# Recurrent heads with tokens on partitions: the norm's factor as a scale per partition, one transpose per block, one fused product

## Chip, core and metric

One core of a Trainium2 chip. The metric is the device time of one execution in microseconds (us); lower is better. TensorE is called PE, VectorE DVE, ScalarE ACT, GpSimd POOL and SyncE SP, as the profile does.

## What is computed

One step of a hybrid encoder layer for 1024 prompt tokens and 32 sample tokens, all in float32: a SwiGLU, a mixing block and a second SwiGLU. The mixing block projects the normalized input once and runs two groups of heads beside each other, a stick-breaking attention (8 heads of 64) and a gated linear recurrence, HGRN2 (4 heads, keys and values of 128 columns). The change lies in the end of the recurrent group:

```python
o_h, S_new = hgrn2_scan(q_h, k_in, heads(hi), log_f, S0, hg_chunk)       # o (B, T, 4, 128)
o_h = rms_norm(o_h, hg_out_gain) * jax.nn.silu(heads(hg))
mix = jnp.concatenate([sb_o, o_h.reshape(B, T, HG_VAL_WIDTH)], axis=-1)
x = x + mix @ w_out
```

`rms_norm` divides each token's 128 values of a head by the root of their mean square and multiplies by a gain per value.

## The kernel before

All 1056 tokens lie on the free axis for most of the program (a tile is 128 features x tokens). Tokens are worked in three groups of columns, 0 to 384, 384 to 768 and 768 to 1056 (`GROUPS`); the last one has 256 prompt and 32 sample tokens.

The mixing block is written as streams that a merger interleaves: the projection (`project_stream`, three products in float32r per pair of tiles, the `pp` rows), and for each of four head pairs the attention (`attend_stream`), the sample's attention (`sample_stream`) and one recurrent head (`hg_stream`). The projection's products are the filler: PE works them off in between, and `behind(g, g.filler)` ties a transpose to the place after the filler product that was written last. From this order a scheduler makes the sequence of each engine, by priorities and its own costs; within an engine everything then runs in that sequence. After the projection, `mix_stream` multiplies by `w_out` in the same way (`ps<-xs_a`), and after all streams `mix_units` adds the last two tiles of features (`ps<-xs_b`).

A recurrent head takes chunks of 128 tokens (8 for the prompt, one of 32 for the sample). For each it makes a new state `S` (a product `pu`, and DVE's update) and the output `po`: `vn` as the weights against `att`, then `S` against `q` (lines 1388 and 1390). The result has the 128 values on partitions and the chunk's tokens on the free axis, and ACT copies it into `f`, whose columns are free by then (line 1391).

The normalization follows in two steps for each group, skewed by one group (`skewed`). `factors` squares a group on ACT (1400), and `token_factors` (207 to 225) transposes the squares on PE in blocks of 128 (216, tile `pmc`), so that a token's squares lie along the free axis; DVE sums them (217), and POOL makes the mean plus epsilon (222) and the power -1/2 (223). `normed` spreads the factor again: `spread` (228) transposes the factor, broadcast over 128 columns, on PE (242, tile `pb`), and DVE multiplies the group by gain and factor (1408) and by the gate `sg` (1410). Then the group is stored in DRAM, or for the last head split into two float32r tiles (`to_xs`).

The attention's outputs `so` are normalized by the same helpers (`sb_out_norm`, 1036): there each token has two heads, and ACT first widens the factors (235, tile `wide`). `token_factors` also makes the factors of queries and keys (`fqn`, `fkn`). Transposes, products `pu` and `po` and several others share the three PSUM banks of the tag `px`.

Of the kernel before, what the change touches and what calls it, by code (L numbers as in the profile page):

```python
# [8 lines left out]
F32 = mybir.dt.float32  # L9
# [137 lines left out]
def gs(n):  # L147
    return slice(*GROUPS[n])


def gw(n):
    return GROUPS[n][1] - GROUPS[n][0]
# [51 lines left out]
EXP_LN, SIGMOID = "natural_log_exp_and_others", "sigmoid_and_others"  # L204


def token_factors(g, f, psp, sq, w, behind_, tokens=None):


    nc = g.nc  # L210
    nb, rows, nh = -(-w // P), min(w, P), f.shape[2]
    mc = psp.tile([P, 3, P], F32, name="pmc", tag="px", bufs=3)
    v = f[0:rows, 0:nb, 0:nh]
    with behind(g, behind_):
        for b in range(nb):
            nc.tensor.transpose(mc[0:rows, b, :], sq[:, b * P:b * P + rows], g.ident)
    nc.vector.tensor_reduce(out=v.rearrange("p b h -> p (b h)"),
                            in_=mc[0:rows, 0:nb, :].rearrange("p b (h d) -> p (b h) d", h=nh), axis=AX.X, op=ALU.add)
    wide = lambda t: t[:, :, None].broadcast_to([rows, nb, nh])
    if tokens is not None:  # L220
        nc.gpsimd.tensor_tensor(out=v, in0=v, in1=wide(g.r2[0:rows, tokens]), op=ALU.mult)
    nc.gpsimd.tensor_scalar(out=v, in0=v, scalar1=nh / P, scalar2=EPS, op0=ALU.mult, op1=ALU.add)
    nc.gpsimd.tensor_tensor(out=v, in0=v, in1=g.mh[0:rows, :, None].broadcast_to([rows, nb, nh]), op=ALU.pow)
    if tokens is not None:
        nc.gpsimd.tensor_tensor(out=v, in0=v, in1=wide(g.rc[0:rows, tokens]), op=ALU.mult)


def spread(g, psp, f, c, w):

    nh, nb = f.shape[2], -(-w // P)  # L230
    rows = min(w, P)
    if nh > 1:
        wide = g.wp.tile([P, TG], F32, name="wide", tag="xp", bufs=3)[0:rows, 0:nb * P]
        wide = wide.rearrange("p (b d) -> p b d", b=nb)
        g.nc.scalar.activation(wide.rearrange("p b (h d) -> p (b h) d", h=nh),
                               f[0:rows, c:c + nb].rearrange("p b h -> p (b h)")[:, :, None]
                               .broadcast_to([rows, nb * nh, P // nh]), AF.Copy)
    pb = psp.tile([P, 512], F32, name="pb", tag="px", bufs=3)
    for b in range(nb):
        rows = min(w - b * P, P)  # L240
        src = wide[0:rows, b] if nh > 1 else f[0:rows, c + b, 0:1].broadcast_to([rows, P])
        g.nc.tensor.transpose(pb[:, b * P:b * P + rows], src, g.ident[0:rows, 0:rows])
    return pb[:, 0:w]
# [1059 lines left out]
def hg_stream(g, m, pool, psp, hh, state, outs, out):  # L1303
# [12 lines left out]
    def cs(b, c):  # L1316
        b0, nch, L = blocks[b]
        return slice(b0 * P + c * L, b0 * P + (c + 1) * L)
# [53 lines left out]
    for b, c in [(0, c) for c in range(8)] + [(1, 0)]:  # L1372
        b0, nch, L = blocks[b]
        kT = kTs[c // 4] if b == 0 else kTs[2]
        vn = v[0:L, b0 + c, :]
        if b == 1:
            nc.sync.dma_start(outs["s_p"][0, 0, hh], S)
            S = S0
        pu = psp.tile([P, 512], F32, name="pu", tag="px", bufs=3)
        nc.tensor.matmul(pu[:, 0:P], kT[:, c % 4, :], vn, start=True, stop=True)  # L1380
        Sn = pool.tile([P, P], F32, name="S", tag="S", bufs=3)
        if S is None:
            nc.vector.tensor_copy(Sn, pu[:, 0:P])
        else:
            nc.vector.scalar_tensor_tensor(out=Sn, in0=S, scalar=f[:, cs(b, c).stop - 1:cs(b, c).stop],
                                           in1=pu[:, 0:P], op0=ALU.mult, op1=ALU.add)
        po = psp.tile([P, 512], F32, name="po", tag="px", bufs=3)
        nc.tensor.matmul(po[:, 0:L], vn, att[b][:, c, :], start=True, stop=(S is None))
        if S is not None:
            nc.tensor.matmul(po[:, 0:L], S, q[:, cs(b, c)], start=False, stop=True)  # L1390
        nc.scalar.activation(f[:, cs(b, c)], po[:, 0:L], AF.Copy)
        S = Sn
        yield 1.0
    nc.sync.dma_start(outs["s_s"][0, 0, hh], S)
    o, fo = f, {}

    def factors(n):
        w = gw(n)
        sq = pool.tile([P, TG], F32, name="sq", tag="sq", bufs=2)
        nc.scalar.activation(sq[:, 0:w], o[:, gs(n)], AF.Square)  # L1400
        if w < TG:
            nc.gpsimd.memset(sq[:, w:TG], 0.0)
        fo[n] = pool.tile([P, 3, 1], F32, name="fh", tag="fh", bufs=3)
        token_factors(g, fo[n], psp, sq, TG, g.filler)

    def normed(n):
        w = gw(n)
        nc.vector.scalar_tensor_tensor(out=o[:, gs(n)], in0=o[:, gs(n)], scalar=g.hgo[:, 0:1],
                                       in1=spread(g, psp, fo[n], 0, w), op0=ALU.mult, op1=ALU.mult)
        nc.vector.tensor_tensor(out=o[:, gs(n)], in0=o[:, gs(n)], in1=sg[:, gs(n)], op=ALU.mult)  # L1410
        out(*GROUPS[n], o[:, gs(n)])

    yield from skewed(factors, normed, range(NG))
# [485 lines left out]
```

## Time and profile before

| | |
|---|---|
| median of 3 runs | 2174.91 us (2167.78 to 2176.68) |
| the profiled execution | 2173.99 us |
| its span | 2172.3 us |
| PE busy | 2118.7 us, 98% of the span |
| DVE, ACT, POOL busy | 1469.8 us (68%), 933.2 us (43%), 585.6 us (27%) |
| granted clock of PE | 0.998 of 2.4 GHz |

Matmuls are pipelined, so a matmul's listed duration is longer than the time by which it moves the next one: what an instruction costs in a stream is read from the starts of its neighbours. In a timeline row the columns are start (us), duration (us), engine, line, operation, output<-input with shapes and number of instructions in a row; in brackets stands the engine's idle time just before and what ended it. A float32 product of 128 x 128 is two instructions, a transpose one. Of a group of instructions the row gives busy time and mean duration (ns) or the least, median and longest duration (ns).

### The profile page before, as it was taken

To read this page: it belongs to the slowest core of one execution; us is meant where nothing else is said; L and a number is where in the kernel's file an instruction comes from. 1 tells how busy PE (TensorE), PEld (TensorE's weight loads), DVE (VectorE), ACT (ScalarE), POOL (GpSimd) and SP (SyncE) were. 2 spreads that over 40 slices of the span, in tenths; PEclk is the share of its full clock that TensorE was granted. 3 is DMA by queue.
4 is the path that set the end of the run, shared out by engine and by line. 5 is a ranking of instruction groups with operands and counts; after the bars stand their busy time and mean duration, and the time that the engine had idled before them with its cause. 6 is when DMAs were issued, how large, how long until landed. Compare 5 with 4: busy or idle time off the path is not lost.

```text
span 2172.3 us, 41486 instructions
## 1 busy us (share of the span) xinstructions
PE 2118.7 (98%) x16331; PEld 2069.1 (95%) x16331; DVE 1469.8 (68%) x2548; ACT 933.2 (43%) x1812; POOL 585.6 (27%) x873
## 2 busy tenths in 40 slices
PE   7999999999999999999999999989999999999998
PEld 7999999999999999989899898989999999999998
DVE  5777666564678558778678688549677666645775
ACT  6433333233446555555564475236223233334443
POOL 1355544341000110311311311121555354320000
PEclk9999999999999999999999999999999999999999
DMA  7565555447535310120121213474775455466343
GB/s 236 179 212 169 153 171 158 155 143 264 202 126 173 106 53 26 44 70 21 54 59 29 66 61 95 142 221 151 234 216 178 158 159 164 162 217 237 122 147 124
DMA packets 328804, 307.28 MB, mean 141 GB/s; under 512 B 26592, under 2 KB 284896, under 8 KB 328608
## 3 DMA queue, kind: packets, MB, share of 16 engines
q1 hardware_dynamic: 259456, 264.75, 37.5%
q10 hardware_dynamic: 68672, 38.25, 6.1%
q8 instruction: 128, 2.10, 0.4%
q0 software_dynamic: 480, 1.62, 0.2%
q14 instruction: 68, 0.56, 0.1%
HBM read 208.46 MB, written 96.11 MB: 140 GB/s over the span
## 4 chain that ended last, share of the span: by engine, by line
PE 53%; DMA 5%; DVE 4%; POOL 1%; ACT 1%; issue 1%; SPq 0%; DVEq 0%; ACTq 0%; POOLq 0%
PE bk L384 16%; PE pp L835 14%; PE bk L699 10%; PE pl L1341 2%; PE ps L1448 2%; PE av L1111 1%; PE pt L1092 1%; DMA xd<-xp 1%; PE ps L1471 1%; PE z L1147 1%; PE z L1146 1%; DMA wraw<-in_ffn_w_in_dram 1%; DMA braw<-in_ffn_w_in_dram 1%; DVE t L1005 1%; DMA oraw<-in_ffn_w_out_dram 1%
## 5 line engine op out<-in xcount | busy, mean ns | idle before, releaser
L699 PE MATMUL bk<-tl,wh 128*128 128x256 f32 x1232 | 349.9, 285 | 0.8 <-DVE tl L657 0.8
L699 PE MATMUL bk<-th,wl 128*128 128x256 f32 x1232 | 349.3, 284 | 0.8 <-DVE wl L646 0.8
L699 PE MATMUL bk<-th,wh 128*128 128x256 f32 x1232 | 348.2, 284 | 0.1
L835 PE MATMUL pp<-xs_a,wh 128*128 128x384 f32 (+1 forms) x1008 | 258.2, 337 | 0.0
L699 PEld LDWEIGHTS bk<-tl,wh 128*128 128x128 f32 x1232 | 231.8, 188 | 1.3 <-DVE tl L657 1.2
L699 PEld LDWEIGHTS bk<-th,wl 128*128 128x128 f32 x1232 | 231.8, 188 | 1.2 <-DVE wl L646 1.0
L699 PEld LDWEIGHTS bk<-th,wh 128*128 128x128 f32 x1232 | 230.9, 188 | 0.8 <-ACT wh L645 0.3
L835 PEld LDWEIGHTS pp<-xs_a,wh 128*128 128x128 f32 x1008 | 168.7, 189 | 6.0 <-issue 4.1
L646 DVE SCALAR_TENSOR_TENSOR wl<-oraw,wh 128x1024 fp32r<-128x1024 f32 x84 | 95.5, 1137 | 107.7 <-ACT wh L645 107.7
L835 PE MATMUL pp<-xs_a,wl 128*128 128x384 f32 (+1 forms) x504 | 164.0, 325 | 0.0
L539 POOL TENSOR_TENSOR gt<-gt,b 128x256 f32<-128x256 f32 x88 | 75.2, 854 | 327.1 <-ACT gt L538 323.0
L645 ACT ACTIVATE wh<-oraw 128x1024 fp32r<-128x1024 f32 x84 | 83.7, 997 | 148.2 <-PE bk L699 128.6
L384 PE MATMUL bk<-ops_a,wh 128*128 128x272 f32 (+1 forms) x704 | 131.8, 287 | 1.3 <-ACT e L364 1.1
L538 ACT ACTIVATE gt<-gt 128x256 f32<-128x256 f32 x88 | 37.3, 424 | 219.7 <-DVE gt L505 219.7
L158 DVE TENSOR_TENSOR wl<-wraw,wh 128x512 fp32r<-128x512 f32 (+2 forms) x126 | 106.5, 859 | 31.6 <-ACT wh L157 31.1
L157 ACT ACTIVATE wh<-wraw 128x512 fp32r<-128x512 f32 (+2 forms) x126 | 89.5, 731 | 88.0 <-PE bk L384 27.8
L384 PEld LDWEIGHTS bk<-ops_a,wh 128*128 128x128 f32 x704 | 110.0, 190 | 2.2 <-ACT e L364 2.2
L543 POOL TENSOR_TENSOR gt<-gt,b 128x256 f32<-128x256 f32 x88 | 88.6, 1007 | 79.7 <-DVE b L505 68.5
L384 PE MATMUL bk<-ops_a,wl 128*128 128x272 f32 (+1 forms) x352 | 100.5, 286 | 0.1
L505 DVE TENSOR_TENSOR gt<-bk,p 128x256 f32<-128x256 f32 (+1 forms) x60 | 25.9, 432 | 110.0 <-PE bk L384 107.7
L835 PEld LDWEIGHTS pp<-xs_a,wl 128*128 128x128 f32 x504 | 94.7, 188 | 0.1
L1003 ACT ACTIVATE t<-z,minus 128x128 f32<-128x128 f32 (+2 forms) x96 | 55.4, 577 | 67.8 <-PE z L1149 48.8
(469 smaller groups left out, 6848.3 us busy)
## 6 DMA issues: line engine op xcount, KB each, us to landing
wraw<-in_ffn_w_in_dram SPq DMA_DIRECT2D x58, 512.0 KB, 4.5
oraw<-in_ffn_w_out_dram SPq DMA_DIRECT2D x94, 256.0 KB, 4.4
sd<-osum SPq DMA_DIRECT2D x44, 512.0 KB, 3.1
gd<-gt SPq DMA_DIRECT2D x42, 528.0 KB, 4.9
braw<-in_ffn_w_in_dram ACTq DMA_DIRECT2D x42, 512.0 KB, 4.3
oraw<-sd SPq DMA_DIRECT2D x40, 512.0 KB, 3.6
oraw<-in_ffn_w_out_dram SPq DMA_DIRECT2D x30, 512.0 KB, 3.3
wraw<-in_w_in_dram SPq DMA_DIRECT2D x28, 512.0 KB, 3.7
```

The lines of the kernel that those rows point to most:

```text
L157: nc.scalar.activation(hi, src, AF.Copy)
L158: return nc.vector.tensor_tensor(out=lo, in0=src, in1=hi, op=ALU.subtract)
L384: mm = g.nc.tensor.matmul(ps, wt[x][:, kk, :], xt[y][:, kk, :], start=(first and kk == 0 and n == 0), stop=(kk == HK - 1 and n == len(PASS ...
L539: nc.gpsimd.tensor_tensor(out=gt[:, 1, cc], in0=gt[:, 1, cc], in1=s["b2"], op=ALU.mult)
L543: last = nc.gpsimd.tensor_tensor(out=gt[:, 0, cc], in0=gt[:, 0, cc], in1=s["b1"], op=ALU.mult)
L645: nc.scalar.activation(h, r, AF.Copy, scale=0.5)
L646: nc.vector.scalar_tensor_tensor(out=l, in0=r, scalar=0.5, in1=h, op0=ALU.mult, op1=ALU.subtract)
L699: nc.tensor.matmul(ps, wt[a][:, d * P:(d + 1) * P], xt[b][:, cols(c)], start=(k == 0 and n == 0), stop=(k == FH - 1 and n == len(PASSES) - 1))
L835: g.filler = nc.tensor.matmul(ps[:, 0:gw(n)], wt[a][:, k, :], xs(b, k)[:, gs(n)], start=(k == 0 and j == 0), stop=(k == KC - 1 and j == le ...
L1003: nc.scalar.activation(a, z, AF.Sigmoid, scale=minus)
L1341: nc.tensor.matmul(pl[0:L, c, 0:hl].rearrange("p (b m) -> p b m", m=m_), k[:, cs(b, c)], qr, start=True, stop=True)
L1448: nc.tensor.matmul(ps[:, 0:w], wt[a][:, k, :], xs(b, c)[:, gs(n)], start=(k == 0 and i == 0), stop=(k == 5 and i == len(PASSES) - 1))
```

## The change

The recurrent output is now made with tokens on partitions: the two products of a chunk exchange their operands, so that `po` holds 128 tokens x 128 values. ACT copies a prompt chunk into the same columns of `f`, and the sample's 32 tokens into a small tile `osm`. The squares of a group are summed by DVE straight from SBUF, without a transpose; POOL makes the factor (`root`, a helper that `token_factors` now calls too); ACT multiplies each block by its factor per partition. In `normed` PE transposes each block back, behind the filler, and DVE multiplies the transposed group from PSUM by gain and gate in one operation. Where a group of 384 columns took 3 + 3 transposes, it now takes 3.

```diff
+def root(g, v, inv_n):
+    g.nc.gpsimd.tensor_scalar(out=v, in0=v, scalar1=inv_n, scalar2=EPS, op0=ALU.mult, op1=ALU.add)
+    g.nc.gpsimd.tensor_tensor(out=v, in0=v, in1=g.mh[0:v.shape[0], :, None].broadcast_to(list(v.shape)), op=ALU.pow)
...
-        nc.tensor.matmul(po[:, 0:L], vn, att[b][:, c, :], start=True, stop=(S is None))
+        nc.tensor.matmul(po[0:L, 0:P], att[b][:, c, :], vn, start=True, stop=(S is None))
         if S is not None:
-            nc.tensor.matmul(po[:, 0:L], S, q[:, cs(b, c)], start=False, stop=True)
-        nc.scalar.activation(f[:, cs(b, c)], po[:, 0:L], AF.Copy)
+            nc.tensor.matmul(po[0:L, 0:P], q[:, cs(b, c)], S, start=False, stop=True)
+        if b == 1:
+            osm = pool.tile([TS, 1, P], F32, name="osm", tag="kTs", bufs=1)[:, 0, :]
+        nc.scalar.activation(osm if b else f[:, cs(b, c)], po[0:L, 0:P], AF.Copy)
...
-    o, fo = f, {}
+    o = f
+    def pieces(n):
+        a, e = GROUPS[n][0], min(GROUPS[n][1], TP)
+        ps = [(o[:, c:c + P], P, c - a) for c in range(a, e, P)]
+        return ps + [(osm, TS, TP - a)] if n == NG - 1 else ps
     def factors(n):
-        w = gw(n)
+        a, e = GROUPS[n][0], min(GROUPS[n][1], TP)
         sq = pool.tile([P, TG], F32, name="sq", tag="sq", bufs=2)
-        nc.scalar.activation(sq[:, 0:w], o[:, gs(n)], AF.Square)
-        if w < TG:
-            nc.gpsimd.memset(sq[:, w:TG], 0.0)
-        fo[n] = pool.tile([P, 3, 1], F32, name="fh", tag="fh", bufs=3)
-        token_factors(g, fo[n], psp, sq, TG, g.filler)
+        nc.scalar.activation(sq[:, 0:e - a], o[:, a:e], AF.Square)
+        if n == NG - 1:
+            nc.gpsimd.memset(sq[:, e - a:TG], 0.0)
+            nc.scalar.activation(sq[0:TS, e - a:TG], osm, AF.Square)
+        fo = pool.tile([P, 3, 1], F32, name="fh", tag="fh", bufs=3)
+        nc.vector.tensor_reduce(out=fo[:, :, 0], in_=sq.rearrange("p (b d) -> p b d", b=3), axis=AX.X, op=ALU.add)
+        root(g, fo[:, :, :], 1.0 / P)
+        for i, (x, rows, _) in enumerate(pieces(n)):
+            nc.scalar.activation(x, x, AF.Copy, scale=fo[0:rows, i, 0:1])
     def normed(n):
-        w = gw(n)
-        nc.vector.scalar_tensor_tensor(out=o[:, gs(n)], in0=o[:, gs(n)], scalar=g.hgo[:, 0:1],
-                                       in1=spread(g, psp, fo[n], 0, w), op0=ALU.mult, op1=ALU.mult)
-        nc.vector.tensor_tensor(out=o[:, gs(n)], in0=o[:, gs(n)], in1=sg[:, gs(n)], op=ALU.mult)
+        pt = psp.tile([P, 512], F32, name="pb", tag="px", bufs=3)
+        with behind(g, g.filler):
+            for x, rows, c in pieces(n):
+                nc.tensor.transpose(pt[:, c:c + rows], x, g.ident[0:rows, 0:rows])
+        nc.vector.scalar_tensor_tensor(out=o[:, gs(n)], in0=pt[:, 0:gw(n)], scalar=g.hgo[:, 0:1], in1=sg[:, gs(n)],
+                                       op0=ALU.mult, op1=ALU.mult)
         out(*GROUPS[n], o[:, gs(n)])
```

Nothing waits for PE between square and factor any more, so the scheduler puts squares, reduction, power and scaling of a group into the loop over the chunks, as soon as the group's chunks are there. Three places show what moves. Lines behind the helper and in `hg_stream` have other numbers after the change (L1398 is the copy of `po`, L1421 the scaling, L1427 the transpose back).

ACT in the first head, from the second group's squares to the copy behind the first `vT`; `cmb` belongs to the attention, `wide<-fqn` to the query factors of the sample. Before:

```order
L1400 ACTIVATE sq<-hf 128x384
L1020 ACTIVATE cmb<-av 64x256
L235 ACTIVATE wide<-fqn 32x128
L1043 ACTIVATE sq<-so 128x384 x2
L947 ACTIVATE vT<-pp 128x384
L1391 ACTIVATE hf<-po 128x128
```

After the change:

```order
L1413 ACTIVATE sq<-hf 128x384
L1421 ACTIVATE hf<-hf,fh 128x128 x2
L1025 ACTIVATE cmb<-av 64x256
L240 ACTIVATE wide<-fqn 32x128
L1048 ACTIVATE sq<-so 128x384 x2
L952 ACTIVATE vT<-pp 128x384
L1398 ACTIVATE hf<-po 128x128
L1421 ACTIVATE hf<-hf,fh 128x128
```

Two scalings of the second group now stand between its squares and the attention's work, the third one behind the next copy of `po`.

PE in the first head, the twelve rows up to the last pair of `wide` (the attention's third group of factors; the sample's 512-column product `zsm` stands some rows ahead). Before:

```order
L835 MATMUL pp<-xs_a,wl 128x384
L835 MATMUL pp<-xs_a,wh 128x384
L216 MATMUL pmc<-ident,sq 128x128 x3
L835 MATMUL pp<-xs_a,wh 128x384
L835 MATMUL pp<-xs_a,wl 128x384
L835 MATMUL pp<-xs_b,wh 128x384 x2
L242 MATMUL pb<-ident,wide 128x128 x3
L835 MATMUL pp<-xs_b,wl 128x384
L835 MATMUL pp<-xs_a,wh 128x384
L242 MATMUL pb<-ident,fh 128x128 x3
L835 MATMUL pp<-xs_a,wh 128x384
L242 MATMUL pb<-ident,wide 128x128 x2
```

After the change:

```order
L840 MATMUL pp<-xs_a,wh 128x384 x2
L840 MATMUL pp<-xs_a,wl 128x384
L840 MATMUL pp<-xs_a,wh 128x384 x2
L222 MATMUL pmc<-ident,sq 128x128 x2
L1427 MATMUL pb<-ident,hf 128x128 x3
L247 MATMUL pb<-ident,wide 128x128 x3
L840 MATMUL pp<-xs_a,wl 128x384
L840 MATMUL pp<-xs_b,wh 128x384 x2
L840 MATMUL pp<-xs_b,wl 128x384
L1427 MATMUL pb<-ident,hf 128x128 x3
L840 MATMUL pp<-xs_a,wh 128x384
L247 MATMUL pb<-ident,wide 128x128 x2
```

The transposes of the scaled output `hf` stand where those of the factor `fh` stood, and of the transposes of squares only the attention's two are left, later than before. From `zsm` to the last pair there are 13 products `pp` (14 before) and 2 transposes of squares (8 before).

PE at the end of the fourth head, where the first products of `mix_units` (`ps<-xs_b`) begin. Before:

```order
L1471 MATMUL ps<-xs_b,lh 128x256 x2
L1471 MATMUL ps<-xs_b,ll 128x256
L1471 MATMUL ps<-xs_b,lh 128x256 x2
L1471 MATMUL ps<-xs_b,ll 128x256
L1471 MATMUL ps<-xs_b,lh 128x256 x2
L1471 MATMUL ps<-xs_b,ll 128x256
L1448 MATMUL ps<-xs_a,wh 128x384 x4
L1471 MATMUL ps<-xs_b,lh 128x256
L1448 MATMUL ps<-xs_a,wl 128x384
```

After the change:

```order
L1490 MATMUL ps<-xs_b,ll 128x256
L1490 MATMUL ps<-xs_b,lh 128x256 x2
L1490 MATMUL ps<-xs_b,ll 128x256
L1490 MATMUL ps<-xs_b,lh 128x256 x2
L1490 MATMUL ps<-xs_b,ll 128x256
L1490 MATMUL ps<-xs_b,lh 128x256 x2
L1490 MATMUL ps<-xs_b,ll 128x256
L1490 MATMUL ps<-xs_b,lh 128x256
L1467 MATMUL ps<-xs_a,wh 128x384 x4
L1467 MATMUL ps<-xs_a,wl 128x384
```

22 products `ps<-xs_b` stand ahead of the four `ps<-xs_a`, where 9 stood (the piece shows the last 12 of them).

## Rows read from the trace of the kernel before

**Rows 1.** The page: busy time of each engine with its share of the span and number of instructions, and PE's granted clock in 40 slices in tenths of full speed.

```profile
PE   2118.7 (98%) x16331; PEld 2069.1 (95%) x16331; DVE 1469.8 (68%) x2548; ACT 933.2 (43%) x1812; POOL 585.6 (27%) x873
...
PEclk9999999999999999999999999999999999999999
```

**Rows 2.** Timeline of PE: the instructions before which it stood still, in heads 1, 2, 3 and 4.

```profile
926.68 0.52 PE L216 MATMUL pmc<-ident,sq 128*128 128x128 f32 x3 [0.33 <-DVE fh L217]
930.29 0.44 PE L242 MATMUL pb<-ident,wide 128*128 128x128 f32 x2 [1.19 <-ACT wide L235]
...
1080.87 0.51 PE L242 MATMUL pb<-ident,fh 128*128 128x128 f32 x3 [0.33 <-DVE so L1049]
1085.29 0.44 PE L242 MATMUL pb<-ident,wide 128*128 128x128 f32 x2 [1.51 <-ACT wide L235]
...
1236.16 0.55 PE L216 MATMUL pmc<-ident,sq 128*128 128x128 f32 x3 [0.26 <-DVE fh L217]
1239.85 0.44 PE L242 MATMUL pb<-ident,wide 128*128 128x128 f32 x2 [1.27 <-ACT wide L235]
...
1405.32 0.54 PE L242 MATMUL pb<-ident,fh 128*128 128x128 f32 x3 [0.58 <-POOL fh L223]
1420.54 1.01 PE L1448 MATMUL ps<-xs_a,wh 128*128 128x384 f32 x4 [2.03 <-ACT wh L157]
```

**Rows 3.** Timelines of PE, ACT, DVE and POOL in head 1: the chain from `zsm` to the copy that the last pair of `wide` waits for.

```profile
922.48 1.07 PE L1208 MATMUL zsm<-KT,qz 128*64 128x512 f32 x2
...
923.72 0.58 ACT L1003 ACTIVATE t<-zsm 64x512 f32<-64x512 f32 x1
...
924.82 1.27 DVE L1005 TENSOR_TENSOR_SCAN t<-t,left,zero 64x512 f32<-64x512 f32 x1
...
926.46 0.67 DVE L1007 TENSOR_TENSOR t<-zsm,t 64x512 f32<-64x512 f32 x1
927.06 0.40 DVE L217 TENSOR_REDUCE fo<-pmc 128x4 f32<-128x256 f32 x1
...
928.18 1.61 POOL L223 TENSOR_TENSOR fo<-fo,mh 128x4 f32<-128x4 f32 x1
...
929.82 0.41 ACT L235 ACTIVATE wide<-fo 128x256 f32<-128x256 f32 x1 [3.75 <-POOL fo L223]
```

**Rows 4.** The transposes of squares as a group of the whole program (busy us, mean ns).

```profile
L216 PE MATMUL pmc<-ident,sq 128*128 128x128 f32 x140 | 23.1, 275 | 0.9 <-DVE fh L217 0.6 <-DVE att L1355 0.3
```

**Rows 5.** Timeline of PE in head 1: projection products of 288 columns before and behind three transposes.

```profile
920.53 0.42 PE L835 MATMUL pp<-xs_a,wh 128*128 128x288 f32 x2
...
920.93 0.49 PE L216 MATMUL pmc<-ident,sq 128*128 128x128 f32 x3
921.17 0.51 PE L835 MATMUL pp<-xs_a,wh 128*128 128x288 f32 x2
...
921.66 0.43 PE L835 MATMUL pp<-xs_b,wh 128*128 128x288 f32 x2
```

**Rows 6.** The recurrent group's operations on DVE and POOL in all four heads (number; least, median and longest ns; first and last start; forms).

```profile
L217 DVE TENSOR_REDUCE fh<-pmc x12: 522/552/558, 922.6 to 1407.0; 128x3 f32<-128x384 f32 x12
...
L1408 DVE SCALAR_TENSOR_TENSOR hf<-hf,hgo,pb x12: 505/596/614, 927.4 to 1411.9; 128x384 f32<-128x384 f32 x8, 128x288 f32<-128x288 f32 x4
...
L1410 DVE TENSOR_TENSOR hf<-hf,hg x12: 445/543/559, 928.4 to 1412.8; 128x384 f32<-128x384 f32 x8, 128x288 f32<-128x288 f32 x4
...
L222 POOL TENSOR_SCALAR fh<-fh x12: 196/196/1102, 923.9 to 1407.7; 128x3 f32<-128x3 f32 x12
...
L223 POOL TENSOR_TENSOR fh<-fh,mh x12: 849/852/1035, 924.2 to 1408.9; 128x3 f32<-128x3 f32 x12
```

**Rows 7.** Timeline of ACT in head 1: copies to a `kos` tile without and with a factor per partition (the second, `rc`), and the stretch from the second group's squares.

```profile
898.26 0.25 ACT L888 ACTIVATE kos<-pns 32x128 f32<-32x128 f32 x1
...
912.64 0.53 ACT L1400 ACTIVATE sq<-hf 128x384 f32<-128x384 f32 x1
914.31 0.38 ACT L1020 ACTIVATE cmb<-av 64x256 f32<-64x256 f32 x1 [1.15 <-PE av L1111]
914.72 0.31 ACT L235 ACTIVATE wide<-fqn 32x128 f32<-32x128 f32 x1
...
933.50 0.34 ACT L888 ACTIVATE kos<-pns,rc 32x128 f32<-32x128 f32 x1
```

**Rows 8.** Timeline of PE in head 1: the transpose of `wide<-fqn`.

```profile
915.27 0.24 PE L242 MATMUL pb<-ident,wide 32*128 32x32 f32 x1
```

**Rows 9.** Timelines of ACT and POOL in head 3.

```profile
1233.42 0.58 ACT L1003 ACTIVATE t<-zsm 64x512 f32<-64x512 f32 x1
...
1231.37 1.32 POOL L223 TENSOR_TENSOR fo<-fo,mh 128x6 f32<-128x6 f32 x1
```

**Rows 10.** Timelines of ACT and PE in head 4: a split of `lraw` and splits that wait behind the loads of `x`, and the first products of `mix_units`.

```profile
1409.21 1.06 ACT L157 ACTIVATE lh<-lraw 128x1024 fp32r<-128x1024 f32 x1 [1.55 <-DMA x<-xd]
...
1418.94 1.13 ACT L157 ACTIVATE xs_b<-hf 128x128 fp32r<-128x128 f32 x5 [8.66 <-DMA x<-xd]
...
1417.53 0.28 PE L1471 MATMUL ps<-xs_b,ll 128*128 128x256 f32 x1
1417.65 0.40 PE L1471 MATMUL ps<-xs_b,lh 128*128 128x256 f32 x2
```

More of the change, by code (lines that the diff above doesn't have):

```diff
@@ L221, in token_factors @@
         nc.gpsimd.tensor_tensor(out=v, in0=v, in1=wide(g.r2[0:rows, tokens]), op=ALU.mult)
-    nc.gpsimd.tensor_scalar(out=v, in0=v, scalar1=nh / P, scalar2=EPS, op0=ALU.mult, op1=ALU.add)
-    nc.gpsimd.tensor_tensor(out=v, in0=v, in1=g.mh[0:rows, :, None].broadcast_to([rows, nb, nh]), op=ALU.pow)
+    root(g, v, nh / P)
     if tokens is not None:
```

## Prediction

> **What bounds the kernel now.** I read first the page's line of engine shares and its clock row: TensorE (PE) is busy in 98% of the span and its granted clock is at the full 2.4 GHz in all 40 slices [rows 1]. So the sum has to be made on PE: its instructions, and the places where it stands still. Then I read the stretches in which the changed code runs, the four heads of the recurrent group between about 900 and 1425 us. The timeline of PE shows where it stands still there. In each of the first three heads it does so twice, within the 10 us that hold the normalization: once for 0.26 to 0.33 us at the transposes that this change removes or moves, and once for 1.19, 1.51 and 1.27 us in front of a pair of transposes of `wide`, which belong to the attention group's normalization and not to this change; the fourth head has 0.58 and 2.03 us [rows 2]. That second wait is the point of this case. It ends with a copy on ScalarE (ACT), which waits for a power on GpSimd (POOL), which waits for a reduction on VectorE (DVE) that stands behind a scan and a product [rows 3]. So in these stretches the thing that ends last is a chain through DVE, POOL and ACT, and PE waits for it in order.
>
> **What the change removes on PE.** Of each group of tokens 3 transposes of `sq` go (12 groups, 36 instructions; the order has 36 fewer on PE). The transposes that spread the factor stay in number: they now carry the scaled output (36 before, 36 now, by the order). The price of three transposes comes from start to start: they start at 920.93 and the next projection product at 921.17, so 0.24 us; and the three products behind them take 0.49 us of PE's stream (921.17 to 921.66) where three undisturbed ones take 0.40 (920.53 to 920.93), so 0.09 more [rows 5]. That is 0.33 us a group and 12 x 0.33 = **4.0 us** of PE time. The group's mean duration in the list, 275 ns [rows 4], would make 36 x 0.275 = 9.9 us; it is a latency, since three of them pass in 0.24 us. The Trainium skill ("TensorE: Matmul & The Clock Gate", Part 4: PE-mode transpose) gives about 275 ns for a transpose in a kernel's context; by that alone the estimate would be the 9.9 us. Taken as the cost in the stream, it is a rival below.
>
> **What it adds on PE.** The products of 128 tokens only exchange their operands, 128 x 128 on both sides: nothing. For the 32 sample tokens the streamed side grows from 32 to 128 columns, in four instructions a head. No row shows the new form. Three products of 288 columns take 0.40 us [rows 5], so 96 more columns cost about 0.40 / 3 x 96 / 288 = 0.045 us, four times that 0.18; between nothing and 0.2 us a head, I take 0.1, so **+0.4 us**.
>
> **DVE and POOL.** DVE loses 12 products of 0.54 us and keeps 12 reductions of 0.55 us, which now read SBUF, and 12 fused products of 0.60 us [rows 6]. No row has the reduction from SBUF; the products of two SBUF operands of the same size take 0.54, so between 0.45 and 0.60, and I take 0.55. These 6.5 us lie beside PE's work and count only where the chain of [rows 3] runs over DVE. POOL's two small operations stay, 0.20 and 0.85 us a group [rows 6]. They, and the reduction, move forward into the loop over the chunks, ahead of the attention group's own factors.
>
> **ACT, where the change adds.** 36 scalings, 128 x 128 with a factor per partition, and 4 more squares. The nearest rows: a 32 x 128 copy with a factor per partition takes 0.34 and one without 0.25 [rows 7]; the squares of 384 columns take 0.53, and the scalings have 128. Bounds 0.25 and 0.53; I take 0.34, the row with the same operand, so 12 us of ACT time, and ACT has room for it. What matters is where they stand. Each scaling waits for reduction, mean and power: 0.55 + 0.20 + 0.85 and some 0.25 us of handing over, 1.85 us after the square ends, and everything behind it in ACT's queue waits too. In heads 1 and 2 the two scalings of the second group stand between the square and `cmb`, `wide<-fqn` and the squares of `so` (the first piece of order). The square ends at 913.17 and `cmb` starts at 914.31, so ACT has 1.15 us of slack there [rows 7]; the scalings end at about 913.17 + 1.85 + 0.6 = 915.6, and `cmb` (0.38) comes 1.3 us later. `wide<-fqn` (0.31) is then done at about 916.3, and PE, which reaches its transpose at 915.27 [rows 8], stands **about 1.0 us**. In head 3 they stand behind the squares of `so`, but the third group's scalings stand ahead of `vT`, the square of `so` and the sigmoid of `zsm`, which begins at 1233.42 today, and they wait for a power that POOL can only start behind the power of `fo` that runs from 1231.37 to 1232.69 [rows 9]: the sigmoid comes up to 1.8 us later, and with it the scan, the reduction of the last `fo` and the wait at the end of [rows 3].
>
> **The sum for heads 1 to 3.** PE needs 1.0 us less of work in each. The chain to the last pair of `wide` now runs from the 512-column `zsm` over sigmoid, scan, a fused product of `so` [rows 6], product and reduction to mean and power and the copy: 1.07 + 0.58 + 1.27 + 0.6 + 0.67 + 0.4 + 1.9 + 0.41, about 6.9 us with nothing in between, against 7.81 us from 922.48 to 930.29 today [rows 2, 3]. PE has fewer instructions to fill it (13 projection products between `zsm` and that pair instead of 14, and 6 fewer `sq` transposes, by the second piece of order). So the 0.9 us that the chain loses are about what `wide<-fqn` and the later sigmoid add in front of it: I take **0 a head**, with -2.3 (all work and both waits gone) and +1.8 as ends. The work that the change saves becomes a longer wait in front of `wide`.
>
> **Head 4 and the way out.** There is no attention work beside it, so three groups save 1.0 us, and the 0.58 us wait for `fh` goes since factors come earlier [rows 2]. Further on PE waits 2.03 us at 1420.54 for a split on ACT that stands behind five splits of `hf`; these begin at 1418.94, when a load of `x` has been let out that waited for a store of `xp` [rows 10]. The order now has 13 more products of 0.12 us in front of that wait (third piece). They would fill 1.6 us of it, but they take two PSUM banks in turn, and the store and the load come no sooner than PE's and DVE's sums before them. I take -0.4 for it, between 0 and -1.6. With 0.1 for the sample chunk, which in heads 1 to 3 is spent where PE waits anyway, that is -1.0 - 0.6 - 0.4 + 0.1 = **-1.9 us**.
>
> **Forecast.** The profiled execution took 2173.99 us, 1.7 more than its span, and 0.9 under the median, 2174.91, of three runs between 2167.78 and 2176.68. 2174.0 + 3 x 0 - 1.9 = **2172 us**. Half a per cent, 10.9 us, is about what a measurement of this kernel can tell from no change.
>
> **Rivals.** *The saving is kept* (0.22): ACT gets through its scalings in its idle time, and PE loses the 4.0 us less 0.4, the waits of 0.33, 0.33, 0.26 and 0.58 and 1.6 at the way out: 6.7 us, 2167.3. For it speaks that ACT is busy for 43% of the span [rows 1]; against it that ACT works in order and that the wait in front of the last `wide` ends on POOL. *A transpose costs its listed duration* (0.06): 9.9 in place of 4.0, so 12.6 and 2161.4; the start to start rows speak against it. *ACT blocks* (0.14), the one that ends slower: the scalings hold up ACT for longer than its slack of 1.15 us, so that `wide<-fqn` and the squares of `so` come late. PE then loses 1.0 in heads 1 and 2 and 1.8 in head 3 on top of an unshortened chain, and 1.6 in head 4, where the second split of `lraw`, which starts after a wait of 1.55 as it is, gets behind them [rows 10]: +5.4, 2179. It decides from the point where a scaling waits for longer than 1.15 us. The Trainium skill ("ScalarE: Activation LUTs", Rules for kernel authors) sends multiplications to VectorE and not to ScalarE; that rule speaks for this rival, but no run here shows the scaling on DVE.
>
> **How the numbers follow.** The forecast has 0.58; its own range is 2169 to 2176. 2163 to 2180 takes in nearly all of it, of the kept saving, and half of the blocking case, and leaves out 2 in 10 with the scatter of the three runs. Faster by more than 10.9 us needs the third case or the kept saving with luck: 0.09. Slower by as much needs a blocked ACT at twice its price: 0.04. Within: 0.87.
>
> **What would show it.** Right: PE has 36 fewer `sq` transposes, ACT 36 scalings of 0.3 to 0.4 us, and PE stands 1.5 to 2.3 us in front of the last `wide` pair of heads 1 to 3, and near 1 us in front of `wide<-fqn` in heads 1 and 2. The kept saving: those waits at 1.2 us or less and none at `wide<-fqn`. ACT blocks: new waits of PE for `hf` or `po`, and a span longer than 2176. The forecast is wrong if the time changes by more than 3 us before 900 us or behind 1475 us, where nothing is computed differently, or if a head of the first three changes by over 2 us.

## The result, and the profile after

The changed kernel takes 2179.10 us (median of 12 runs, 2176.89 to 2185.16) against 2175.26 for the kernel before (median of 12): a ratio of 1.0025, 95% interval 1.0014 to 1.0035. It is **slower** by 3.8 us, where the forecast had 2172 and the likeliest sign was a gain. 2179 is also the number of the rival *ACT blocks*, but by another sum: it added 5.4 to a base of 2174.0, where 3.8 was measured.

The page of the changed kernel: busy time of each engine, and PE's granted clock in 40 slices. They answer to [rows 1].

```profile
PE   2120.9 (97%) x16295; PEld 2069.8 (95%) x16295; DVE 1466.6 (67%) x2536; ACT 945.7 (43%) x1852; POOL 588.3 (27%) x873
...
PEclk9999999999999999999999999999999999999999
```

PE has 36 instructions fewer and is not less busy; the span is 2179.2 us in place of 2172.3. Of these 6.9 us 4.3 lie behind the second norm (from the start of the last `ms<-rr,ones` on), where nothing is computed differently; in the thirteen profiles of this study that stretch takes anything from 700.6 to 706.5 us, so the medians and the stretch of the change are what counts. To see where, one needs a mark that both traces have. Each head begins its chunks with a copy of the first state, `S<-pu` on DVE. The row of the group gives the first and the last of the four starts; first before, then after:

```profile
L1383 DVE COPY S<-pu x4: 279/286/292, 899.4 to 1376.3; 128x128 f32<-128x128 f32 x4
```

```profile
L1388 DVE COPY S<-pu x4: 280/286/292, 899.8 to 1380.3; 128x128 f32<-128x128 f32 x4
```

From the first to the last mark lie the normalizations of heads 1 to 3: 476.9 us before and 480.5 after, **+3.6 us**, about the size of the measured loss. By the single starts the three heads take 154.55, 157.83 and 164.51 us before, 156.14, 159.32 and 165.02 after. Timeline of PE in the changed kernel, the instructions before which it stood still in heads 1, 2 (first two), 3 and 4; these rows answer to [rows 2, 8]:

```profile
910.97 0.49 PE L1393 MATMUL po<-hvn,att 128*128 128x128 f32 x2 [0.38 <-ACT hf L1398]
917.60 0.24 PE L247 MATMUL pb<-ident,wide 32*128 32x32 f32 x1 [1.17 <-ACT wide L240]
927.05 0.55 PE L247 MATMUL pb<-ident,wide 128*128 128x128 f32 x3 [0.48 <-ACT wide L240]
929.44 0.52 PE L247 MATMUL pb<-ident,wide 128*128 128x128 f32 x3 [0.32 <-DVE so L1054]
932.10 0.44 PE L247 MATMUL pb<-ident,wide 128*128 128x128 f32 x2 [0.94 <-ACT wide L240]
...
1067.11 0.49 PE L1393 MATMUL po<-hvn,att 128*128 128x128 f32 x2 [0.40 <-ACT hf L1398]
1073.74 0.24 PE L247 MATMUL pb<-ident,wide 32*128 32x32 f32 x1 [1.17 <-ACT wide L240]
...
1239.04 0.46 PE L222 MATMUL pmc<-ident,sq 128*128 128x128 f32 x2 [1.86 <-ACT sq L1048]
...
1408.15 0.24 PE L247 MATMUL pb<-ident,wide 32*128 32x32 f32 x1 [2.43 <-ACT wide L240]
```

Head 1 had two waits, 1.52 us in all [rows 2]; it now has five, 3.29 us, and four of them end with a copy on ACT. The timelines of ACT and POOL around the second and the third group of head 1 say what ACT was doing. The first three ACT rows answer to [rows 7], where `cmb` came 1.15 us after the square with nothing in between:

```profile
913.75 0.53 ACT L1413 ACTIVATE sq<-hf 128x384 f32<-128x384 f32 x1
916.12 0.69 ACT L1421 ACTIVATE hf<-hf,fh 128x128 f32<-128x128 f32 x2 [1.84 <-POOL fh L210]
916.83 0.38 ACT L1025 ACTIVATE cmb<-av 64x256 f32<-64x256 f32 x1
917.23 0.31 ACT L240 ACTIVATE wide<-fqn 32x128 f32<-32x128 f32 x1
...
925.26 0.69 ACT L1421 ACTIVATE hf<-hf,fh 128x128 f32<-128x128 f32 x2 [1.90 <-POOL fh L210]
...
926.50 0.51 ACT L240 ACTIVATE wide<-fo 128x384 f32<-128x384 f32 x1
926.91 0.57 ACT L1008 ACTIVATE t<-zsm 64x512 f32<-64x512 f32 x1
...
915.23 0.86 POOL L210 TENSOR_TENSOR fh<-fh,mh 128x3 f32<-128x3 f32 x1
...
924.38 0.85 POOL L210 TENSOR_TENSOR fh<-fh,mh 128x3 f32<-128x3 f32 x1
```

ACT stands idle for 1.84 and 1.90 us in front of a scaling and starts it when POOL's power is done. For part of that time the work behind it is ready: `cmb`, which needed 1.15 us after the square in [rows 7], comes 2.55 us after it here. The scalings then take 0.39 us each, and `cmb`, `wide` and the sigmoid `t<-zsm` come that much later. In head 3 it is the third group, behind two powers in a row on POOL:

```profile
1235.07 1.32 POOL L210 TENSOR_TENSOR fo<-fo,mh 128x6 f32<-128x6 f32 x1
...
1236.76 0.85 POOL L210 TENSOR_TENSOR fh<-fh,mh 128x3 f32<-128x3 f32 x1
...
1237.64 0.69 ACT L1421 ACTIVATE hf<-hf,fh 128x128 f32<-128x128 f32 x2 [3.37 <-POOL fh L210]
...
1238.58 0.41 ACT L1048 ACTIVATE sq<-so 128x256 f32<-128x256 f32 x1
```

ACT waits 3.37 us, the square of `so` behind it comes at 1238.58, and PE, which needs it, stands for 1.86. What follows on PE was in no part of the prediction. Three stretches of that head, with length, PE's busy time, granted clock, DMA share and GB/s; then PE's rows in the second stretch:

```profile
1230.00:1239.00 9.00, 7.14 (x44) 1.00 0.11 35
1239.30:1242.70 3.40, 3.40 (x15) 0.50 0.00 0
1242.70:1246.00 3.30, 3.30 (x22) 0.99 0.60 217
```

```profile
1239.80 0.99 PE L840 MATMUL pp<-xs_a,wh 128*128 128x384 f32 x2
1240.59 0.52 PE L840 MATMUL pp<-xs_a,wl 128*128 128x384 f32 x1
1240.90 0.84 PE L840 MATMUL pp<-xs_a,wh 128*128 128x384 f32 x2
1241.55 0.52 PE L840 MATMUL pp<-xs_a,wl 128*128 128x384 f32 x1
...
1245.36 0.51 PE L840 MATMUL pp<-xs_a,wh 128*128 128x384 f32 x2
1245.71 0.33 PE L840 MATMUL pp<-xs_a,wl 128*128 128x384 f32 x1
```

Right behind the wait the granted clock goes from 2.4 to 1.2 GHz for 3.4 us, and two products of 384 columns take 0.65 us (1240.90 to 1241.55) where they take 0.35 at 1245.36. Had the work of these 3.4 us gone at 0.35 for such a pair, it would have taken about 1.8, so the fall costs about 1.6 us; that is an estimate from these rows. The slices of the page, 54 us each, do not show it: a 9 there means 90% or more. The kernel before also has two stretches at 1.2 GHz, from 46.9 and from 101.5 us, which its row of nines does not show and the prediction did not see; they lie far from the change.

### The profile page after: what moved, and what is told of

The parts are those of the page before. It is cut to its first block, busy times and chain, and to the rows that moved or that the text cites. A ratio compares the mean times of both kernels' runs of the same rounds, so it can differ in the third digit from the quotient of the medians.

```text
span 2179.2 us, 41425 instructions
## 1 busy us (share of the span) xinstructions
PE 2120.9 (97%) x16295; PEld 2069.8 (95%) x16295; DVE 1466.6 (67%) x2536; ACT 945.7 (43%) x1852; POOL 588.3 (27%) x873
## 4 chain that ended last, share of the span: by engine, by line
PE 53%; DVE 4%; DMA 3%; POOL 2%; ACT 2%; issue 1%; SPq 0%; DVEq 0%; POOLq 0%; ACTq 0%
PE bk L389 17%; PE pp L840 13%; PE bk L704 10%; PE ps L1467 3%; PE pl L1346 2%; PE av L1116 1%; PE pt L1097 1%; PE ps L1490 1%; PE z L1152 1%; PE z L1151 1%; DVE t L1010 1%; PE pb L247 0%; DMA oraw<-in_ffn_w_out_dram 0%; PE pmc L222 0%; DMA out_dram<-y 0%
```

## The experiments

Three theories stood against each other. **A, the place in the queue:** ACT works in order, a scaling waits for its power, and what stands behind it is late. **B, the chain:** the chain from `zsm` to the last pair of `wide` sets the end of each head, so that saved PE work turns into waiting (the forecast's reason for 0 a head). **C:** the heads do not matter, the clock and the way out do. The table has 12 timed runs of each kernel (11 of u1 and u3, 9 of t4) beside runs of the kernel before; "heads" is the time from the first to the last `S<-pu` in the one profiled run.

| kernel | heads 1 to 3, us | median, us | ratio to before |
|---|---|---|---|
| before | 476.9 | 2175.3 to 2176.2 | 1 |
| changed | 480.5 | 2179.10 | 1.0025 (1.0014 to 1.0035) |
| s1 scalings behind squares of `so` | 471.6 | 2172.43 | 0.9978 (0.9968 to 0.9988) |
| s2 on DVE | 475.2 | 2177.02 | 1.0003 (0.9992 to 1.0014) |
| s3 not waiting | 471.9 | 2171.45 | 0.9977 (0.9967 to 0.9987) |
| s4 without scalings | 472.3 | 2172.71 | 0.9981 (0.9969 to 0.9993) |
| t1 s1 in heads 1 to 3, changed in 4 | 471.9 | 2172.96 | 0.9983 (0.9974 to 0.9993) |
| t2 s1 in heads 1 to 3, before in 4 | 471.5 | 2170.84 | 0.9977 (0.9966 to 0.9988) |
| t3 changed in head 4 alone | 476.3 | 2175.98 | 0.9998 (0.9986 to 1.0011) |
| t4 changed in heads 1 to 3 alone | 480.7 | 2183.03 | 1.0035 (1.0023 to 1.0047) |
| u1 t2 with 27 transposes added | 474.3 | 2176.64 | 1.0000 (0.9990 to 1.0010) |
| u2 on POOL, before in head 4 | 476.8 | 2175.40 | 0.9998 (0.9984 to 1.0011) |
| u3 t4 with group 2 of heads 1, 2 late | 476.9 | 2175.77 | 0.9993 (0.9985 to 1.0002) |

### s1: the same scalings, later in ACT's queue

```diff
 def sb_out_norm
-        nc.scalar.activation(sq[:, 0:cw], o[:, c:c + cw], AF.Square)
+        g.copied = nc.scalar.activation(sq[:, 0:cw], o[:, c:c + cw], AF.Square)
 hg_stream: from factors(n) into normed(n), ahead of the transposes
+        with behind(g, g.copied):
+            for i, (x, rows, _) in enumerate(pieces(n)):
+                nc.scalar.activation(x, x, AF.Copy, scale=fos[n][0:rows, i, 0:1])
```

> The changed kernel with one thing moved: in ACT's queue the scalings of a group stand behind the last squares of the attention's output `so` that were written, so that no attention work waits behind a scaling that waits for its power. Same instructions, same count. Theory A (place in the queue): PE's waits of 1.17 us in front of the 32x32 transpose of wide in heads 1 and 2, of 0.38 in front of po, and of 1.86 in head 3 go; the wait in front of the last pair of wide comes back to 1 to 2 us; the time goes from 2179.1 to 2173 to 2176. Theory B (the chain from zsm sets the end whatever ACT does before it, and saved PE work turns into waiting): the sum of PE's waits in a head stays at 3.0 to 3.5 us, only at another place, and the time stays at 2178 to 2180. Theory C (it is the clock and the way out, not the heads): heads as in A or B, but the time stays within 1.5 us of 2179.

2172.43, a little under A's range, 6.7 us under the changed kernel and faster than before. Timeline of PE, the waits of heads 1 to 3 (they are all that the three normalizations have) and one of head 4:

```profile
930.57 0.44 PE L247 MATMUL pb<-ident,wide 128*128 128x128 f32 x2 [0.86 <-ACT wide L240]
...
1083.62 0.44 PE L247 MATMUL pb<-ident,wide 128*128 128x128 f32 x2 [0.86 <-ACT wide L240]
...
1236.13 0.44 PE L247 MATMUL pb<-ident,wide 128*128 128x128 f32 x2 [0.52 <-ACT wide L240]
...
1415.65 0.33 PE L1429 MATMUL pb<-ident,hf 128*128 128x128 f32 x1 [2.61 <-ACT hf L1425]
```

And of ACT, from the second group's square to the scalings of the first group, with the sigmoid of `zsm` (its product starts at 924.10 on PE):

```profile
914.27 0.53 ACT L1413 ACTIVATE sq<-hf 128x384 f32<-128x384 f32 x1
915.95 0.38 ACT L1025 ACTIVATE cmb<-av 64x256 f32<-64x256 f32 x1 [1.15 <-PE av L1116]
916.35 0.31 ACT L240 ACTIVATE wide<-fqn 32x128 f32<-32x128 f32 x1
...
925.36 0.58 ACT L1008 ACTIVATE t<-zsm 64x512 f32<-64x512 f32 x1
...
926.66 0.98 ACT L1425 ACTIVATE hf<-hf,fh 128x128 f32<-128x128 f32 x3
```

`cmb` is back at its place, 1.15 us after the square as in [rows 7], and no scaling waits for a power any more. Heads 1 to 3 gain 5.3 us on the kernel before, with fewer and shorter waits (0.86 us at the last pair, where A had 1 to 2): A, not B. In head 4 the scalings now stand behind DMA issues, and PE waits 2.61 us for one.

### s2, s3, s4: another engine, no wait, no scaling

```diff
-            nc.scalar.activation(x, x, AF.Copy, scale=fo[0:rows, i, 0:1])
+            nc.vector.tensor_scalar(out=x, in0=x, scalar1=fo[0:rows, i, 0:1], scalar2=None, op0=ALU.mult)   # s2
+            nc.scalar.activation(x, x, AF.Copy, scale=g.hgo[0:rows, 0:1])                                    # s3
```

s4 has neither line.

> The changed kernel with the 36 scalings on DVE in place of ACT. Theory A: the 1.17 us in front of the 32x32 transpose of wide go in heads 1 and 2, but the scalings now stand ahead of an update of S and of `so<-av` on DVE and wait for the same powers, so that PE waits for pu or po by about 1 us a head: 2174 to 2178. Theory B: as the changed kernel, 2178 to 2180. A pure matter of ACT's busy time (12 us moved away from it, and DVE faster at it) would give 2172 or less.

> The changed kernel with the scalings multiplying by the gain tile in place of the factor, so that the normalization of the recurrent output is left out; reduction and power still run. ACT has the same 36 scalings of 0.39 us, but none waits for a power. Theory A: waits of PE at wide<-fqn under 0.3 us and the 1.86 of head 3 gone; 2172 to 2175. Theory B: still 3.0 us and more of waits in each of the heads 1 and 2, 2178 to 2180. If ACT's added busy time is what costs, the waits shrink by less than half: 2176 to 2178.

> The changed kernel without the 36 scalings (the recurrent output stays unnormalized). Theory A: within 1.0 us of the run in which the scalings wait for nothing, 2171 to 2175. If ACT's busy time costs: at least 1.5 us less than that run. Theory B: 2177 to 2180. In each case the wait in front of the last pair of wide in heads 1 to 3 shows what the chain from zsm takes by itself; if it stays over 1.5 us, the 4 us of PE work that the change saves are not to be had in these heads.

s3 is the cleanest of the three: ACT does the same 36 scalings at the same length, and the heads take 471.9 in place of 480.5. The row of s3 (32 of the 36), then that of the changed kernel:

```profile
L1421 ACT ACTIVATE hf<-hf,hgo x32: 385/389/404, 904.0 to 1392.6; 128x128 f32<-128x128 f32 x32
```

```profile
L1421 ACT ACTIVATE hf<-hf,fh x32: 385/387/404, 909.8 to 1414.2; 128x128 f32<-128x128 f32 x32
```

s4, without them, is not faster than s3 (472.3 and 2172.71; A had the two within 1.0 us of each other). So 14 us of ACT's busy time cost nothing, and the waiting in ACT's queue costs 8.6 us of the heads, with the fall of the clock that comes with it. On DVE a scaling takes 0.283 us (median) and the hold-up is smaller but there: 475.2. It lies in one head. Heads 1 and 2 take 153.2 and 156.4 us, as in s1 (153.1 and 156.2), without the waits for `pu` or `po` that the expectation had; head 3 takes 165.65 in place of 162.39, because there DVE waits 1.25 and 2.48 us for powers in front of scalings, and PE stands 0.93, 0.98 and 0.72 us for reductions and products of DVE that come behind them. The Trainium skill ("ScalarE: Activation LUTs", Rules for kernel authors) sends `mul` to VectorE; the trace agrees that the instruction is shorter there (0.283 against 0.387). But the place in the queue decided more than the engine: late on ACT beats DVE by 3.6 us in the heads, 3.3 of them in head 3.

### t1 to t4: which heads

The form and the place of the scalings are chosen by head; nothing else differs.

> Heads 1 to 3 with the scalings behind the last squares of `so`, head 4 exactly as in the changed kernel. From the update that starts head 1's chunks to that of head 4 the run with all four heads moved took 471.6 us (before 476.9, changed 480.5), but from there to the sums of the second norm 95.3 against 92.4 before and 90.8 in the changed kernel, with a wait of 2.61 us for a scaling. Theory A (each head's scalings cost what waits behind them): the 4 us of head 4 come back, 2166 to 2170. Rival (the way out is a matter of the clock, and differs from run to run): 2171 to 2173.

> Heads 1 to 3 with the scalings behind the last squares of `so`, head 4 as before the change. Theory A: 5.3 us less than before, from the three heads alone: 2169 to 2171.5. If head 4's new form is worth its 1.6 us, this is 1 to 2 us behind the run that has it. Rival (clock): what PE gains in the heads is lost to a clock that falls more often, 2173 to 2176.

> The changed form in head 4 alone, heads 1 to 3 as before. The prediction had -1.9 us for this part, the profile of the changed kernel shows -1.6 up to the second norm. Theory A: 2172.5 to 2175. Rival (the 2.43 us in front of the 32x32 transpose of wide and the fall of the clock behind it belong to this part and cost more than it saves): 2176 to 2179.

> Heads 1 to 3 exactly as in the changed kernel, head 4 as before. Theory A: the whole loss sits here, +3.6 us from the waits behind the scalings: 2178 to 2180.5, and PE shows the waits of 1.17 in heads 1 and 2 and of 1.9 in head 3 again. Rival (the loss is in the clock behind 1400 us): 2174.5 to 2177.

t4 speaks against C: heads 1 to 3 lose 3.8 us in it (480.7), with the same waits and the same fall of the clock at 1240 us, and heads 1 and 2, which have no such fall, lose 1.6 and 1.3 of them. As the whole account C is out; as a part it stays, since the fall in head 3 is the clock's, and t4 has 3.1 us more behind the heads. t2 has the gain of the same heads with the scalings late, 2170.84, the lowest median (by ratio level with s1 and s3). The totals missed twice: t4 came out over its 2178 to 2180.5 although its heads did what A said, and t3 between its two ranges. For head 4 the runs therefore say little: t3's ratio, 0.9998 (0.9986 to 1.0011), agrees with nothing and with the forecast's -1.9 alike; t1 missed its 2166 to 2170, lies in its rival's 2171 to 2173, and is no better than t2. The time behind the last `S<-pu` is not held down by these kernels: t2, t4, u1, u2 and u3 share their order in head 4 and behind, and their medians stand 0.1 over, 3.1 over, 3.0 over, 0.7 under and 0.4 under what heads 1 to 3 would give. Part of it is the clock. In the profiled runs the stretch from the last `S<-pu` to the last `ms<-rr,ones` has no time at 1.2 GHz in the kernel before, s2, s3 and u3, 3.4 us in u2, 6.8 in the changed kernel, t2, t3 and t4, and 10.2 in s1, s4, t1 and u1. With its 6.8 the changed kernel still takes 1.5 us less there than the one before (92.9 against 94.4), and t3 1.1 us more (95.4). What brings these falls, and the rest of the scatter, stays open.

### u1: the PE work put back

```diff
+        mc = psp.tile([P, 3, P], F32, name="pmc", tag="px", bufs=3)
+        with behind(g, g.filler):
+            for i in range(3):
+                nc.tensor.transpose(mc[:, i, :], g.ident, g.ident)
```

> The kernel with late scalings in heads 1 to 3 and head 4 as before (2170.8 us; 471.5 us from the first update of head 1 to that of head 4), with three transposes of the identity added on PE per group of tokens, 27 in all, whose result nobody reads: the PE work that the change removed in these heads, without its waits. By the price of the prediction, 0.33 us for three, 9 x 0.33 = 3.0 us: 474.5, and 2173.8. By their own starts alone, 0.08 each: 2.2 us, 473.7. If the chain from zsm sets the end of each head, the waits of 0.86, 0.86 and 0.52 us in front of the last pair of wide take in the added work: 0 to 0.8 us, 471.5 to 472.3. By the listed duration of 275 ns: 7.4 us, 478.9.

Heads 474.3 against 471.5 for t2: 2.8 us for 27 transposes, 0.31 for three; the forecast had 0.33. The median, 2176.64, is 2.8 over the sum's 2173.8, and the heads are not where that comes from. PE's waits in front of the last pair of `wide`, 0.86, 0.86 and 0.52 us in t2, are shorter in u1:

```profile
926.17 0.44 PE L247 MATMUL pb<-ident,wide 128*128 128x128 f32 x2 [0.35 <-ACT wide L240]
...
1080.66 0.44 PE L247 MATMUL pb<-ident,wide 128*128 128x128 f32 x2 [0.75 <-ACT wide L240]
...
1234.21 0.44 PE L247 MATMUL pb<-ident,wide 128*128 128x128 f32 x2 [0.36 <-ACT wide L240]
```

So the waits took in 0.8 us of the added work, and the work itself was 3.6 us, 0.40 for three. The row of these transposes lists 0.27 us for each:

```profile
L1439 PE MATMUL pmc<-ident x27: 270/272/332, 919.9 to 1231.7; 128*128 128x128 f32 x27
```

That would have made 7.4 us. The Trainium skill ("TensorE: Matmul & The Clock Gate", Part 4: PE-mode transpose) has about 275 ns in a kernel's context, measured on bf16; the trace agrees with that as a listed duration, also for float32. u1 shows that a transpose costs the stretch 0.10 us, or 0.13 with what the waits took in. They took in a fifth of the work and not all of it, as B would have it.

### u2, u3: POOL, and one group alone

u2 has `nc.gpsimd.tensor_scalar` for the scalings of heads 1 to 3; u3 moves those of group 2 behind the squares of `so` in heads 1 and 2, and leaves the others.

> Heads 1 to 3 as in the changed kernel but with the scalings on POOL, where they follow the power on the same engine; head 4 as before. On ACT the same three heads took 480.5 us, on DVE 475.2, late on ACT 471.5. Theory A (what counts is who stands behind the scalings): on ACT and DVE nothing waits for them any more, and on POOL the powers of fqn and fo stand behind three scalings of about 0.4 us: up to 1.3 us a head, 472 to 476 us in all, 2171 to 2175.5. Rival (early scalings cost what they cost on any engine): 479 or more, 2178 and more.

> Heads 1 to 3 as in the changed kernel and head 4 as before, but in heads 1 and 2 the scalings of the second group alone stand behind the squares of `so`; those of the first and third group stay where the change put them. With all of them early the heads took 156.1, 159.2 and 165.4 us. Theory A (hold-ups add up): the waits of 1.17 in front of the 32x32 transpose go and nothing comes in their place: 154.9 and 158.0, 478.2 in all. Theory B (an early wait is taken out of a later one, since the chain from zsm sets the end; the forecast's reason for 0 a head): the last wait grows by as much, 156 and 159 stay. A third outcome, more than 1.5 us less a head, would say that the early wait also delays what the later ones wait for.

u2 lands at 476.8, over its range of 472 to 476 and under the rival's 479: the second power of `fo` stands behind three scalings on POOL, which take 2.95 us in head 1, and PE waits 2.09 us for `wide<-fo` in heads 1 and 2. In head 1 3.4 us at 1.2 GHz follow that wait. u3 gives 154.33 and 157.50 for heads 1 and 2 where t4 has 156.10 and 159.16: **1.8 and 1.7 us less** for a wait of 1.15 that went. Timeline of PE in u3, head 1 to the last pair, and of t4 from `zsm` to that pair:

```profile
910.50 0.49 PE L1398 MATMUL po<-hvn,att 128*128 128x128 f32 x2 [0.38 <-ACT hf L1403]
...
923.07 1.07 PE L1213 MATMUL zsm<-KT,qz 128*64 128x512 f32 x2
...
925.34 0.55 PE L247 MATMUL pb<-ident,wide 128*128 128x128 f32 x3 [0.47 <-ACT wide L240]
927.72 0.52 PE L247 MATMUL pb<-ident,wide 128*128 128x128 f32 x3 [0.33 <-DVE so L1054]
930.39 0.44 PE L247 MATMUL pb<-ident,wide 128*128 128x128 f32 x2 [0.42 <-ACT wide L240]
```

```profile
925.10 1.07 PE L1213 MATMUL zsm<-KT,qz 128*64 128x512 f32 x2
...
932.43 0.44 PE L247 MATMUL pb<-ident,wide 128*128 128x128 f32 x2 [0.94 <-ACT wide L240]
```

By its number this is the third outcome, and the rows show where the time goes. From the mark to `zsm` head 1 takes 1.3 us less (23.7 against 25.0): the chain begins with a product on PE, so a wait of PE ahead of it delays all of the chain. From `zsm` to the last pair nothing changes (7.32 against 7.33), which is the part of B that holds: the chain sets the length of that stretch. The last wait falls from 0.94 to 0.42 because the new order puts 16 projection products there in place of 13, and they are missing behind the pair, where the last 0.5 us are gained. An early hold-up is not taken out of a later wait.

## Why the prediction was wrong

- **The price of the transposes: right in size.** 0.33 us for three; u1 measured 0.31, or 0.40 with what the waits took in. The listed 275 ns as a cost in the stream fell, as argued.
- **The pieces on DVE, POOL and ACT: right in size.** In the changed kernel the reduction from SBUF takes 0.549 (0.55 was taken), the power 0.85, a scaling 0.387 (0.34 taken, bounds 0.25 and 0.53).
- **The wait at `wide<-fqn`: right.** 1.17 us in heads 1 and 2; about 1.0 was forecast, and by the same steps: the scalings end 2.5 us after the square (914.28 to 916.81), with 2.45 in the working.
- **The sum for heads 1 to 3: the step that failed.** It put the hold-ups at 1.0, 1.0 and 1.8 and set them against "the 0.9 us that the chain loses", for 0 a head. Both sides were too small. First the hold-ups: the changed kernel minus s1 gives them as 3.1, 3.2 and 2.6 us, 8.8 in place of 3.8. Only the second group's was priced in heads 1 and 2; the copy of `po` behind the first group's scalings (0.38) and `wide<-fo` and the sigmoid behind the third group's were not. That sigmoid begins 2.13 us after the start of `zsm` (924.78 to 926.91), in s1 1.26, and the chain takes 7.32 us in place of s1's 6.47. In head 3 the 1.86 us have the cause that the forecast named (a power of `fo` ahead of that of `fh`), but PE stands in front of the transposes of `so`'s squares and not of the last pair, and the fall of the clock is on top. Second the chain: without hold-ups it loses more than 0.9. From the start of `zsm` to the last pair s1 takes 6.5 us in head 1 (924.10 to 930.57; the estimate was 6.9, before 7.81), and in the three heads 1.3, 1.8 and 2.0 us less than before, nearly all of the 1.5, 1.7 and 2.1 us that the heads gain. "The work that the change saves becomes a longer wait" did not come true: PE waits 0.86 us there in s1 and 0.94 in the changed kernel, not 1.5 to 2.3.
- **Head 4 and the way out: not settled.** -1.9 was forecast. In the profiled run the waits of 0.58 and 2.03 went [rows 2], and one of 2.43 came, on ACT behind DMA issues that wait for a store of `xp`. t3's ratio, 0.9998, cannot be told from -1.9 or from no change. One of the prediction's own signs of being wrong came up, 4.3 us more behind the second norm; as that stretch scatters by 5.9 us, it says nothing about the change.
- **The rivals.** *ACT blocks* (0.14) named the mechanism. That its numbers fit is luck: it had 1.0, 1.0 and 1.8 in heads 1 to 3 on an unshortened chain, 3.8 in all, and the +3.6 measured are 1.6, 1.5 and 0.5, made of 8.8 of hold-ups less 5.3 of saving. Its 1.6 in head 4 was not seen: the split of `lraw` there did not hold PE up. Its condition, a scaling that waits longer than 1.15 us, was met in the forecast's own working (1.85 us after the square). *The saving is kept* is what s1, s3 and t2 do: 5.0 to 5.4 us in heads 1 to 3, where its terms make 3.6.

## What to carry to other kernels

An operation that is cheap and off the critical engine is not free when it has to wait: what it costs is what stands behind it in an in-order queue, so follow every instruction behind it up to the one that the bound engine waits for. A hold-up of the bound engine ahead of the instruction that starts a chain is not absorbed by a wait at the chain's end; unless both are shown to run in parallel, add them. And before moving work to another engine, try the same instruction later in the same queue: here that turned +3.6 us into -5.3 in the stretch concerned.

## What the runs showed of the hardware

- Granted clock: in the changed kernel, t4 and u3 a wait of 1.86 us of PE in head 3 was followed each time by 3.4 us at 1.2 GHz; s1, s2, s3, s4, t1 and t2, without that wait, had no fall there. But the same wait does not always bring it: in u2 a wait of 2.09 us in head 1 did (the stretch below: 0.52 granted), the equal one in head 2 did not. A wait of 2.5 us in front of a product `ps<-xs_b`, between 1455 and 1472 us, stands in all thirteen profiles, and in eight of them the clock fell within 1.5 us of its end. A wait can so cost more than its length.

```profile
924.90:927.00 2.10, 0.04 (x1) 1.00 0.25 94
927.00:930.40 3.40, 3.37 (x14) 0.52 0.31 116
```

- Over the timed runs the mean granted clock was 0.9949 for the changed kernel and 0.9966 to 0.9970 for the one before; but s1, which is 6.7 us faster than the changed kernel, has 0.9949 too, so this mean ranks no kernels.
- POOL: a scaling of 128 x 128 took 0.61 us there (median of 24), against 0.39 on ACT and 0.28 on DVE.
